# The opening of a transformer block kernel: instructions issued in written order on four engines

## The chip, the cores and the metric

The kernel runs on one core of a Trainium2 chip. A core has five engines with a queue each: PE (TensorE, matrix products into PSUM), DVE (VectorE), ACT (ScalarE), POOL (GpSimd) and SP (which here only issues the DMAs that bring data from HBM into SBUF). Each engine works its queue in the order in which the program was compiled, and an instruction whose inputs or buffers aren't ready holds everything behind it on that engine. The metric is the time of one execution on the device, in microseconds (us); lower is better.

## The reference, cut to what matters

The reference is one layer of a diffusion transformer block on two streams of 256 tokens (context and latent) with 1024 channels. The part that the change touches is the start of the first feed-forward layer:

```
mod = silu(c) @ w_ada + b_ada             # 9 vectors of 1024 for each stream
shift, scale, gate, ... = split(mod, 9)
h = rmsnorm(x) * norm * (1 + scale) + shift
a, b = split(h @ w13, 2)                  # w13: 1024 x 5632
x = x + 0.5 * gate * ((silu(a) * b) @ w2)
```

After it come the rest of this layer, retention and Fourier mixing, the merge, a second feed-forward layer and a final norm. All data are float32.

## The kernel before, in words

Channels lie on the 128 partitions, so the 1024 channels are eight tiles, and the 512 tokens of both streams lie along the free axis. A float32 product is made of three products of rounded numbers (the helper `mm3`, lines 86 to 90): weights and activations are each split into a high part (a cast on ACT, `wh`, `h1h`) and a low part (a subtraction on DVE, `wl`, `h1l`), and PE adds low times high (L88), high times low (L89) and high times high (L90).

The opening (lines 96 to 333) does the following.

- SP loads a unit matrix, the small vectors `sm`, the conditioning vectors `cr`, the tokens `xs` in four DMAs of two channel tiles, and then for each channel tile k two 128x1024 tiles of `w_ada` (`ada`, one for the scale, one for the shift) and the first columns of `w13` (`w`, 128x768).
- The conditioning vectors go through SiLU, are split and are spread over all partitions by products with ones (L158) into `cb`; transposed, they are `ct` (L164, L167).
- The norm: the squares of the eight tiles (L227 on DVE, L229 on ACT) in the four rotating buffers of tag t2k, their sums by products with ones (L231, `st`), a square root on ACT (L216, `sd1q`), a reciprocal on DVE (L218, `rstd1q`), and four products that spread it to all partitions (L238, `rs`), copied by ACT (L242, `rstd`).
- For each channel tile, the scale by DVE: a multiply with a running sum of `ada` with `cb`, once for each stream (L181, `junk`), then L190 (`amul`). The shift by PE: eight transposes of the other `ada` tile (L252, `tr`), two ACT copies (L255, `at`), products with `ct` (L258), an ACT copy (L263, `row`), a product with two columns (L264) and a DVE addition (L265, `mod`).
- Then the tile itself: DVE multiplies it with scale and rstd (L289, `xr`), ACT adds the shift and rounds (L292, `h1h`), DVE makes the low part (L293, `h1l`).
- With that, 18 products for each tile into six accumulators (`acc`, three pairs of hidden units); eight tiles make them complete. `first_mod` (L314) and the loop at L321 trace these steps.

The written order isn't the order of the queues. The program is compiled by a scheduler that simulates the engines and picks, whenever an engine is free in that simulation, a ready instruction. So the queues of all engines were set by it, DMAs included. After the opening come the hidden units from number 3 on (`ffn1_up`, 48 products each, `pa` and `pb`), which need `h1h` and `h1l` of all eight tiles, two loads and splits of `w13` each (L77 to L79), and go on beside the remaining `ada` tiles on DVE.

Of the kernel before, what the change touches and what calls it, by code (L numbers as in the profile page):

```python
# [13 lines left out]
P = 128  # L14
T = 256
# [22 lines left out]
def block_kernel(ctx: ExitStack, tc: tile.TileContext, i: dict, out: bass.AP):  # L38
# [28 lines left out]
    def wtile(t, name):  # L67
        return wp.tile([P, 1024], F32 if t == "wr" else F32R, name=name, tag=t, bufs=4)
# [29 lines left out]
    pools = {}  # L98
    cr = wtile("wr", "cr")[:, :512]
    V.memset(cr, 0.0)  # L100
    nc.sync.dma_start(cr.rearrange("(q r) n -> q r n", r=32)[:, 0, :], i["cc"])
    unit_raw = stp.tile([P, P], F32, name="unit_raw")
    nc.sync.dma_start(unit_raw, i["unit"])
    sm = per.tile([P, N_SMALL], F32, name="sm")
    nc.sync.dma_start(sm, i["smalls"])
    ones = per.tile([P, P], F32, name="ones")
    V.memset(ones, 1.0 / D)
    ones_dv = per.tile([P, P], F32, name="ones_dv")
    V.memset(ones_dv, 1.0 / DV)
# [26 lines left out]
    first_loads(0)  # L136
    first_loads(1)


    pick = stp.tile([P, 512], F32, name="pick")  # L140
    V.memset(pick, 0.0)
    for q in range(4):
        V.memset(pick[32 * q : 32 * q + 1, q * P : (q + 1) * P], 1.0)
    one_f = wtile("wr", "one_f")[:, :P]
    V.memset(one_f, 1.0)
    one_r = wtile("wh", "one_r")[:, :P]
    V.tensor_copy(one_r, one_f)
# [6 lines left out]
    for q in range(4):  # L154
        r = slice(32 * q, 32 * q + 1)
        ps = bank(f"cb{q}")
        for n, c in enumerate(ch):
            PE.matmul(ps, one_r[r, :], c[r, :], start=(n == 0), stop=(n == 1), tile_position=(32 * q, 0))  # L158
        (S.copy if q % 2 else V.tensor_copy)(cb[:, q // 2, (q % 2) * 512 : (q % 2 + 1) * 512], ps)
    ct = stp.tile([P, 2, 4, 32], F32, name="ct")  # L160
    V.memset(ct, 0.0)
# [7 lines left out]
    both = stp.tile([P, 2], F32, name="both")  # L169
    for st in range(2):  # L170
        V.tensor_reduce(
            both[:, st : st + 1], unit_raw.rearrange("p (q r) -> p r q", r=32)[:, st, :],
            axis=mybir.AxisListType.X, op=ALU.add,
        )
# [47 lines left out]

    ps_st = bank("st1")
    for k in range(KT):
        sq = tp.tile([P, 512], F32, name=f"sq1_{k}", tag="t2k", bufs=T2K)
        if k % 3 == 1:
            V.tensor_tensor(sq, xs[k], xs[k], op=ALU.mult)  # L227
        else:
            S.activation(sq, xs[k], AF.Square)  # L229
        for q in range(4):  # L230
            PE.matmul(  # L231
                ps_st[32 * q : 32 * q + 32, :P], ones[:, :32], sq[:, q * P : (q + 1) * P],
                start=(k == 0), stop=(k == KT - 1), skip_group_check=True, tile_position=(0, 32 * q),
            )
# [6 lines left out]
    rstd1 = stp.tile([P, 512], F32, name="rstd1")  # L241
    S.copy(rstd1, ps_st)  # L242

    def ada_pe(n):


        raw = first_ada.pop(n)
        tr = [bank(f"tr{n}_{j}") for j in range(2)]
        at = [stp.tile([P, 512], F32, name=f"at{n}_{j}", tag=f"at{j}") for j in range(2)]
        for j in range(2):  # L250
            for c in range(4):
                PE.transpose(  # L252
                    tr[j][:, c * P : (c + 1) * P], raw[:, (4 * j + c) * P : (4 * j + c + 1) * P], unit_raw
                )
            S.copy(at[j], tr[j])  # L255
        for j in range(2):
# [6 lines left out]
        S.copy(row, tr[1][:, :P])  # L263
        PE.matmul(tr[0][:, :2], row, both, start=True, stop=True)  # L264
        V.tensor_scalar(  # L265
            mod[:, :, n : n + 1].rearrange("p s o -> p (s o)"), tr[0][:, :2],
            sm[:, BIAS + n : BIAS + n + 1], None, op0=ALU.add,
        )

    def modulated(dst, st, s, k, rstd, col, name, engine=None, lo=None):  # L270

        w = rstd.shape[-1]
        if w > T:
            xr = stp.tile([P, 512], F32, name=f"xr{name}", tag="xr", bufs=2)
        else:
            xr = tp.tile([P, 512], F32, name=f"xr{name}", tag="t2k", bufs=T2K)
# [34 lines left out]
        split(gg[0], gg[1], sa)  # L311
        return gg

    def first_mod(k):  # L314
        ada(KT + k)
        ada_pe(k)
        scale_cols(0, k, k + 1)

    first_mod(0)
    acc = [bank(f"acc{m}") for m in range(2 * M1)]  # L320
    for k in range(KT):  # L321
        if k + 2 < KT:
            first_loads(k + 2)
        modulated(h[k], 0, (0, 1), k, rstd1, 0, f"1_{k}")
        n = 2 * M1 * P
        hi, lo = wtile("wh", f"wh0_{k}"), wtile("wl", f"wl0_{k}")
        S.copy(hi[:, :n], first_w[k][:, :n])
        V.tensor_tensor(lo[:, :n], first_w[k][:, :n], f32(hi[:, :n]), op=ALU.subtract)
# [720 lines left out]
```

## Time and profile before

| | |
|---|---|
| Time, median of 3 runs (lowest, highest) | 1023.95 us (1022.84, 1025.29) |
| The profiled execution: its time, its span | 1024.28 us, 1022.5 us |
| PE busy | 983.2 us, 96% of the span |
| DVE, ACT, POOL busy | 661.5 us (65%), 469.1 us (46%), 62.3 us (6%) |
| Chain that ended last, by engine | PE 89%, DVE 4%, ACT 3%, issue 1%, DMA 1% |

The span is what the profiler recorded; the execution's time is 1.78 us longer. PE is the engine that is nearly always busy. The stretches in which it is not are the start, three places between the stages, and the last 10 us. A share of busy time over the whole span doesn't tell what a stage is worth: that is read from the rows of the stage.

### The profile page before, as it was taken

How to read it: one execution, taken by the hardware profiler on the slowest of the kernel's cores; microseconds unless marked ns; L12 is line 12 of the kernel's file. 1: busy time of each engine (PE TensorE's matmuls, PEld its weight loads, DVE VectorE, ACT ScalarE, POOL GpSimd, SP SyncE). 2: the span in 40 equal slices, each digit the busy share in tenths (PEclk: the TensorE clock that was granted, in tenths of full speed). 3: DMA queues.
4: the chain of work that ended last, by engine and by line, in shares of the span. 5: the costliest groups of instructions: out<-in, count | busy, mean ns of one | idle time of the engine just before them, and what ended most of it. 6: DMA issues, size and time to landing. Idle time of an engine off the chain costs nothing.

```text
span 1022.5 us, 16777 instructions
## 1 busy us (share of the span) xinstructions
PE 983.2 (96%) x6792; PEld 907.0 (89%) x6792; DVE 661.5 (65%) x1083; ACT 469.1 (46%) x725; POOL 62.3 (6%) x39
## 2 busy tenths in 40 slices
PE   4899999999999999999999998999999989999996
PEld 3668888888888889899999997999999989999995
DVE  7938999998332434875575637955555767667543
ACT  5444232223422423755476457754445545554541
POOL 0000000000000013100000007000000210000011
PEclk9999999999999999899999999999999999999999
DMA  8727766996232233224132625455666555656651
GB/s 345 246 76 250 226 208 197 317 409 235 83 111 70 86 89 110 83 85 125 60 124 63 201 65 163 125 172 187 197 186 187 165 164 171 186 181 174 185 179 42
DMA packets 49238, 166.84 MB, mean 163 GB/s; under 512 B 5380, under 2 KB 7044, under 8 KB 49160
## 3 DMA queue, kind: packets, MB, share of 16 engines
q1 hardware_dynamic: 49160, 165.77, 50.8%
q8 instruction: 53, 0.87, 0.3%
q14 instruction: 25, 0.20, 0.1%
HBM read 164.70 MB, written 1.05 MB: 162 GB/s over the span
## 4 chain that ended last, share of the span: by engine, by line
PE 89%; DVE 4%; ACT 3%; issue 1%; DMA 1%; POOL 0%; SPq 0%; DVEq 0%; ACTq 0%; POOLq 0%
PE y L88 4%; PE y L89 4%; PE y L90 4%; PE pa L88 3%; PE pa L89 3%; PE pb L89 3%; PE pa L90 3%; PE pb L90 3%; PE pb L88 3%; PE ro L89 2%; PE ro L90 2%; PE ro L88 2%; PE fa L89 2%; PE z L90 2%; PE z L88 2%; PE z L89 2%
## 5 line engine op out<-in xcount | busy, mean ns | idle before, releaser
L79 DVE TENSOR_TENSOR wl<-wr,wh 128x1024 fp32r<-128x1024 f32 (+1 forms) x214 | 249.0, 1164 | 203.0 <-ACT wh L78 202.1
L78 ACT CAST wh<-wr 128x1024 fp32r<-128x1024 f32 (+1 forms) x226 | 226.9, 1005 | 281.6 <-PE y L90 79.2
L181 DVE CUSTOM_DVE_ANT_0 junk<-ada,cb,sm 128x1024 bf16<-128x1024 f32 x96 | 122.8, 1280 | 5.3 <-DMA ada<-in_ada 4.5
L89 PE MATMUL y<-gl,wh 128*128 128x512 f32 (+1 forms) x198 | 72.5, 366 | 0.0
L88 PE MATMUL y<-gh,wl 128*128 128x512 f32 (+1 forms) x198 | 72.4, 366 | 0.0
L90 PE MATMUL y<-gh,wh 128*128 128x512 f32 (+1 forms) x198 | 72.3, 365 | 0.0
L379 POOL TENSOR_TENSOR ssum<-ssum,sq 128x256 f32<-128x256 f32 (+1 forms) x18 | 24.5, 1362 | 736.0 <-ACT sq L378 722.8
L88 PE MATMUL pa<-h1h,wl 128*128 128x512 f32 x152 | 59.2, 390 | 0.0
L89 PE MATMUL pa<-h1l,wh 128*128 128x512 f32 x152 | 59.1, 389 | 0.0
L90 PE MATMUL pa<-h1h,wh 128*128 128x512 f32 x152 | 59.1, 389 | 0.0
L88 PE MATMUL pb<-h1h,wl 128*128 128x512 f32 x152 | 59.1, 389 | 0.0
L89 PE MATMUL pb<-h1l,wh 128*128 128x512 f32 x152 | 59.1, 389 | 0.0
L90 PE MATMUL pb<-h1h,wh 128*128 128x512 f32 x152 | 59.1, 389 | 0.0
L89 PE MATMUL fa<-hxl,wh 128*128 128x258 f32 x176 | 50.9, 289 | 0.0
L88 PE MATMUL fa<-hxh,wl 128*128 128x258 f32 x176 | 50.8, 289 | 0.0
L90 PE MATMUL fa<-hxh,wh 128*128 128x258 f32 x176 | 50.6, 288 | 0.0
L89 PE MATMUL fb<-hxl,wh 128*128 128x258 f32 x176 | 50.1, 284 | 0.0
L89 PE MATMUL z<-g2l,wh 128*128 128x256 f32 x176 | 50.0, 284 | 0.0
L88 PE MATMUL fb<-hxh,wl 128*128 128x258 f32 x176 | 50.0, 284 | 0.0
L90 PE MATMUL fb<-hxh,wh 128*128 128x258 f32 x176 | 49.9, 283 | 0.0
L88 PE MATMUL z<-g2h,wl 128*128 128x256 f32 x176 | 49.8, 283 | 0.0
L90 PE MATMUL z<-g2h,wh 128*128 128x256 f32 x176 | 49.8, 283 | 0.0
(309 smaller groups left out, 2896.5 us busy)
## 6 DMA issues: line engine op xcount, KB each, us to landing
ada<-in_ada SPq DMA_DIRECT2D x72, 512.0 KB, 5.2
wr<-in_w13b SPq DMA_DIRECT2D x44, 512.0 KB, 4.4
wr<-in_w13a SPq DMA_DIRECT2D x38, 512.0 KB, 4.2
wrv<-in_wv SPq DMA_DIRECT2D x16, 512.0 KB, 4.5
wr<-in_wg SPq DMA_DIRECT2D x16, 512.0 KB, 3.8
wr<-in_wgate SPq DMA_DIRECT2D x16, 512.0 KB, 4.4
wr<-in_pret SPq DMA_DIRECT2D x16, 512.0 KB, 3.7
wr<-in_w2b SPq DMA_DIRECT2D x16, 512.0 KB, 3.6
```

The lines of the kernel that those rows point to most:

```text
L78: S.copy(hi[:, :n], raw[:, :n])
L79: (lo_engine or V).tensor_tensor(lo[:, :n], raw[:, :n], f32(hi[:, :n]), op=ALU.subtract)
L88: PE.matmul(o, w[1], a[0], start=start, stop=False)
L89: PE.matmul(o, w[0], a[1], start=False, stop=False)
L90: PE.matmul(o, w[0], a[0], start=False, stop=stop)
L181: V.tensor_tensor_reduce(junk, raw, cb[:, s, :], 1.0, sm[:, BIAS + n : BIAS + n + 1], ALU.mult, ALU.add, mod[:, s, n : n + 1],)
L379: G.tensor_tensor(ssum[0][:, cols], ssum[0][:, cols], sq[:, :w], op=ALU.add)
```

## The change

All of the opening is put under a manual schedule for PE, ACT, DVE and SP: on these four engines its instructions stand in the order in which the code issues them, where before the scheduler chose. What comes after the opening is still placed by the scheduler, which may set single instructions between. The code is written in another order to go with that:

- The loads: the unit matrix, `cr`, `xs`, the first `ada` and `w` tiles, then `sm`, then tile by tile.
- The squares alternate between ACT and DVE and have eight buffers (the four of t2k, and four that belong to tiles used later: at0, at1 and two of xr). The copies of `cb` stand between the first squares; the constant `pick` is written after the squares.
- The steps of a channel tile are functions of their own. For the tile after next no work is done ahead any more: beside the products of tile k, the transposes, rows, scale, weight split and columns of tile k + 1 are issued at fixed places between them.

```diff
+    opening = ExitStack()
+    opening.enter_context(
+        tc.manual_schedule(
+            engines={
+                mybir.EngineType.PE, mybir.EngineType.Activation, mybir.EngineType.DVE, mybir.EngineType.SP
+            }
+        )
+    )
...
+        if k < T2K:
+            sq = tp.tile([P, 512], F32, name=f"sq1_{k}", tag="t2k", bufs=T2K)
+        else:
+            sq = stp.tile([P, 512], F32, name=f"sq1_{k}", tag=f"at{k % 2}" if k < 6 else "xr", bufs=1 + (k > 5))
-        if k % 3 == 1:
+        if k % 2:
             V.tensor_tensor(sq, xs[k], xs[k], op=ALU.mult)
...
+        if k == 1:
+            cb_copy(0, V.tensor_copy)
+            cb_copy(1, S.copy)
...
-    S.copy(rstd1, ps_st)
+    for s in range(2):
+        S.copy(rstd1[:, s * T : (s + 1) * T], ps_st[:, s * T : (s + 1) * T])
...
-    first_mod(0)
+    ada_turn(0)
+    first_scaled(0)
+    first_split(0)
+    ada_rows(0)
+    ada_cols(0)
+    first_shifted(0)
     acc = [bank(f"acc{m}") for m in range(2 * M1)]
     for k in range(KT):
         if k + 2 < KT:
             first_loads(k + 2)
-        modulated(h[k], 0, (0, 1), k, rstd1, 0, f"1_{k}")
...
-        if k + 1 < KT:
-            first_mod(k + 1)
-        for n in range(2 * M1):
-            mm3(acc[n], sl((hi, lo), slice(None), slice(n * P, (n + 1) * P)), h[k], k == 0, k == KT - 1)
+        more = k + 1 < KT
+        if more:
+            ada_turn(k + 1)
+        first_products(k, range(0, 2))
+        if more:
+            ada_rows(k + 1)
+            first_scaled(k + 1)
+            first_split(k + 1)
+        first_products(k, range(2, 4))
+        if more:
+            ada_cols(k + 1)
+            first_shifted(k + 1)
+        first_products(k, range(4, 6))
+    V.memset(ones_dv, 1.0 / DV)
+    opening.close()
     start.close()
```

`ada_turn` holds the transposes and the `at` copies, `ada_rows` the products with `ct` and the `row` copy, `ada_cols` the last product and `mod`; `first_scaled` is `junk` (twice), `amul` and `xr`, `first_split` is `wh` and `wl`, `first_shifted` is `h1h` and then `h1l`.

ACT, from the square roots of the norm to the first `h1h`, before (numbers behind a name are the scheduler's buffer numbers, those directly behind `wh_` the channel tile):

```order
L327 CAST wh_1_354<-w_1_115 128x768
L216 ACTIVATE sd1q<-st_162,eps 128x128
L327 CAST wh_2_420<-w_2_279 128x768
L327 CAST wh_3_486<-w_3_345 128x768
L242 COPY rstd_220<-rs_215 128x512
L255 COPY at_0_244<-tr_0_242 128x512
L255 COPY at_1_245<-tr_1_243 128x512
L255 COPY at_0_298<-tr_0_296 128x512
L263 COPY row_264<-tr_1_243 128x128
L255 COPY at_1_299<-tr_1_297 128x512
L263 COPY row_318<-tr_1_297 128x128
L292 ACTIVATE h1h_222<-xr_0_281,mod 128x256 x2
```

and the same place now:

```order
L242 ACTIVATE sq_4_182<-xs_110 128x512
L242 ACTIVATE sq_6_194<-xs_112 128x512
L226 ACTIVATE sd1q<-st_153,eps 128x128
L266 COPY rstd_217<-rs_216 128x256 x2
L280 COPY at_0_242<-tr_0_240 128x512
L280 COPY at_1_243<-tr_1_241 128x512
L351 CAST wh_0_262<-w_0_118 128x768
L293 COPY row_274<-tr_1_241 128x128
L371 ACTIVATE h1h_224<-xr_0_259,mod 128x256 x2
```

The casts of weight tiles 1 to 3 and the copies for tile 1 have gone from between the norm and the first `h1h`; the cast of tile 0 has come in.

PE, the start of one step (products of tile 3, transposes for tile 4), before:

```order
L252 MATMUL tr_0_494<-unit_raw,ada_409 128x128 x4
L252 MATMUL tr_1_495<-unit_raw,ada_409 128x128 x4
L88 MATMUL acc_269<-h1h_228,wl_3_487 128x512
L88 MATMUL acc_270<-h1h_228,wl_3_487 128x512
L88 MATMUL acc_271<-h1h_228,wl_3_487 128x512
L88 MATMUL acc_272<-h1h_228,wl_3_487 128x512
L88 MATMUL acc_273<-h1h_228,wl_3_487 128x512
L88 MATMUL acc_274<-h1h_228,wl_3_487 128x512
L258 MATMUL tr_1_495<-at_0_496,ct 32x128 x4
L258 MATMUL tr_1_495<-at_1_497,ct 32x128 x4
L89 MATMUL acc_269<-h1l_229,wh_3_486 128x512
L90 MATMUL acc_269<-h1h_228,wh_3_486 128x512
```

and one step now (products of tile 2, transposes for tile 3):

```order
L277 MATMUL tr_0_426<-unit_raw,ada_356 128x128 x4
L277 MATMUL tr_1_427<-unit_raw,ada_356 128x128 x4
L88 MATMUL acc_282<-h1h_228,wl_2_399 128x512
L89 MATMUL acc_282<-h1l_229,wh_2_398 128x512
L90 MATMUL acc_282<-h1h_228,wh_2_398 128x512
L88 MATMUL acc_283<-h1h_228,wl_2_399 128x512
L89 MATMUL acc_283<-h1l_229,wh_2_398 128x512
L90 MATMUL acc_283<-h1h_228,wh_2_398 128x512
L288 MATMUL tr_1_427<-at_0_428,ct 32x128 x4
L288 MATMUL tr_1_427<-at_1_429,ct 32x128 x4
L88 MATMUL acc_284<-h1h_228,wl_2_399 128x512
L89 MATMUL acc_284<-h1l_229,wh_2_398 128x512
```

Before, the last product of the shift (L264) comes after all 18 products of a step, just ahead of the next transposes; now it (L299) comes after the twelfth, with six products behind it.

DVE in one step, before (here the scales of tiles 5 and 6 stand beside the weight split of tile 5 and the `mod` and `h1l` of tile 2):

```order
L190 TENSOR_SCALAR amul<-mod,sm 128x2
L181 ISA junk_0_556,mod<-ada_473,cb,sm 128x1024
L181 ISA mod 128x1
L181 ISA junk_1_558,mod<-ada_473,cb,sm 128x1024
L181 ISA mod 128x1
L265 TENSOR_SCALAR mod<-tr_0_362,sm 128x2
L328 TENSOR_TENSOR wl_5_619<-w_5_477,wh_5_618 128x768
L190 TENSOR_SCALAR amul<-mod,sm 128x2
L181 ISA junk_0_622,mod<-ada_539,cb,sm 128x1024
L181 ISA mod 128x1
L293 SCALAR_TENSOR_TENSOR h1l_227<-xr_2_413,mod,h1h_226 128x256 x2
```

and one step now:

```order
L191 ISA junk_0_588,mod<-ada_486,cb,sm 128x1024
L191 ISA mod 128x1
L191 ISA junk_1_590,mod<-ada_486,cb,sm 128x1024
L191 ISA mod 128x1
L200 TENSOR_SCALAR amul<-mod,sm 128x2
L364 SCALAR_TENSOR_TENSOR xr_5_593<-xs_110,amul,rstd_217 128x256 x2
L352 TENSOR_TENSOR wl_5_597<-w_5_490,wh_5_596 128x768
L300 TENSOR_SCALAR mod<-tr_0_558,sm 128x2
L374 SCALAR_TENSOR_TENSOR h1l_235<-xr_5_593,mod,h1h_234 128x256 x2
```

Every DVE instruction of a step now belongs to the one tile whose products come next, and each step has the same nine rows.

## Rows read from the trace of the kernel before

**Rows 1.** Windows: busy us of each engine, granted clock, DMA share, GB/s.
```profile
0.00:29.15 29.15, 13.88 (x137) 9.94 (x137) 22.03 (x50) 15.30 (x26) 0.21 (x4) 1.00 0.91 351
29.15:74.95 45.80, 41.85 (x283) 31.84 (x283) 29.65 (x63) 17.85 (x36) 0.00 (x0) 1.00 0.45 149
75.00:200.00 125.00, 125.00 (x553) 103.51 (x553) 115.35 (x183) 39.09 (x51) 0.00 (x0) 1.00 0.73 232
```

**Rows 2.** Waits of PE, 0 to 75 us: total, times, longest.
```profile
PE acc L88 <- ACT h1h L292: 4.1, 6, 0.9
PE rs L238 <- DVE rstd1q L218: 3.7, 1, 3.7
```

**Rows 3.** Timeline of PE, opening: start, duration, instruction, idle before.
```profile
15.63 1.23 PE L231 MATMUL st<-sq,ones 128*32 128x128 f32 x16 [1.93 <-ACT sq L229]
20.61 2.08 PE L238 MATMUL rs<-rstd1q,pick 128*128 128x128 f32 x8 [3.74 <-DVE rstd1q L218]
22.48 2.93 PE L252 MATMUL tr<-unit_raw,ada 128*128 128x128 f32 x16
...
29.15 1.66 PE L88 MATMUL acc<-h1h,wl 128*128 128x512 f32 x6 [0.50 <-ACT h1h L292]
```

**Rows 4.** Timeline of ACT, opening.
```profile
6.37 0.63 ACT L229 ACTIVATE sq<-xs 128x512 f32<-128x512 f32 x1 [0.47 <-DMA xs<-in_xs]
7.63 1.15 ACT L229 ACTIVATE sq<-xs 128x512 f32<-128x512 f32 x2 [0.64 <-DMA xs<-in_xs]
...
18.18 0.36 ACT L216 ACTIVATE sd1q<-st,eps 128x128 f32<-128x128 f32 x1
...
28.19 0.91 ACT L292 ACTIVATE h1h<-xr,mod 128x256 fp32r<-128x256 f32 x2
```

**Rows 5.** Timeline of DVE, opening.
```profile
1.74 0.48 DVE L141 MEMSET pick<- 128x512 f32 x1
...
2.74 0.85 DVE L143 MEMSET pick<- 1x128 f32 x4
...
11.88 1.29 DVE L159 COPY cb<-cb 128x512 f32<-128x512 f32 x2 [0.78 <-PE cb L158]
...
18.74 0.95 DVE L328 TENSOR_TENSOR wl<-w,wh 128x768 fp32r<-128x768 f32 x1
19.61 0.94 DVE L218 RECIPROCAL rstd1q<-sd1q 128x128 f32<-128x128 f32 x1
...
27.93 0.22 DVE L265 TENSOR_SCALAR mod<-tr,sm 128x2 f32<-128x2 f32 x1
```

**Rows 6.** Timeline of PE, one step and the end of the steps.
```profile
41.56 1.63 PE L88 MATMUL acc<-h1h,wl 128*128 128x512 f32 x6 [0.65 <-ACT h1h L292]
...
46.73 1.11 PE L252 MATMUL tr<-unit_raw,ada 128*128 128x128 f32 x8
...
74.95 0.47 PE L88 MATMUL pa<-h1h,wl 128*128 128x512 f32 x1
```

**Rows 7.** Timeline of DVE, the parts of a step.
```profile
37.44 1.29 DVE L181 CUSTOM_DVE_ANT_0 junk<-ada,cb,sm 128x1024 bf16<-128x1024 f32 x1
...
38.77 1.28 DVE L181 CUSTOM_DVE_ANT_0 junk<-ada,cb,sm 128x1024 bf16<-128x1024 f32 x1
...
49.12 0.88 DVE L293 SCALAR_TENSOR_TENSOR h1l<-xr,mod,h1h 128x256 fp32r<-128x256 f32 x2
49.91 0.22 DVE L190 TENSOR_SCALAR amul<-mod,sm 128x2 f32<-128x2 f32 x1
50.04 0.88 DVE L289 SCALAR_TENSOR_TENSOR xr<-xs,amul,rstd 128x256 f32<-128x256 f32 x2
```

**Rows 8.** Windows, behind a pause of PE between two stages.
```profile
412.00:416.00 4.00, 3.96 (x16) 3.60 (x17) 4.00 (x6) 1.51 (x3) 2.62 (x1) 0.50 0.25 98
416.00:420.00 4.00, 4.00 (x32) 3.90 (x32) 3.37 (x8) 3.13 (x7) 0.00 (x0) 0.86 0.48 135
```

**Rows 9.** DMA issues, 0 to 60 us: KB each, median us to landing.
```profile
w<-in_w13a SPq DMA_DIRECT2D x8, 384.0 KB, 8.3
```

More of the change, by code (lines that the diff above doesn't have):

```diff
@@ L98, in block_kernel @@
     pools = {}
+    unit_raw = stp.tile([P, P], F32, name="unit_raw")
+    nc.sync.dma_start(unit_raw, i["unit"])
     cr = wtile("wr", "cr")[:, :512]
@@ L101, in block_kernel @@
     nc.sync.dma_start(cr.rearrange("(q r) n -> q r n", r=32)[:, 0, :], i["cc"])
[L102 to L109, printed above, removed]
     eps = per.tile([P, 1], F32, name="eps")
@@ L113, in block_kernel @@
     S.activation(warm, eps, AF.Silu)
+    ones = per.tile([P, P], F32, name="ones")
+    V.memset(ones, 1.0 / D)
+    one_f = wtile("wr", "one_f")[:, :P]
+    V.memset(one_f, 1.0)
+    one_r = wtile("wh", "one_r")[:, :P]
+    V.tensor_copy(one_r, one_f)
+    ct = stp.tile([P, 2, 4, 32], F32, name="ct")
+    V.memset(ct, 0.0)
+    both = stp.tile([P, 2], F32, name="both")
+    for st in range(2):
+        V.tensor_reduce(
+            both[:, st : st + 1], unit_raw.rearrange("p (q r) -> p r q", r=32)[:, st, :],
+            axis=mybir.AxisListType.X, op=ALU.add,
+        )
+    sm = per.tile([P, N_SMALL], F32, name="sm")
+    ones_dv = per.tile([P, P], F32, name="ones_dv")
     mod = per.tile([P, 2, 72], F32, name="mod")
@@ L136, in block_kernel @@
     first_loads(0)
+    nc.sync.dma_start(sm, i["smalls"])
     first_loads(1)
[L140 to L147, printed above, removed]
     cb = adp.tile([P, 2, D], F32, name="cb")
@@ L153, in block_kernel @@
     S.activation(warm, cr[:, :1], AF.Sqrt, bias=eps, scale=0.0)
[L154 to L161, printed above, removed]
     ps = bank("ct")
@@ L167, in block_kernel, with cb_copy @@
         V.tensor_copy(ct[:, :, :, st], picked[:, st, :, :, 0])
[L169 to L174, printed above, removed]
+    cb_ps = []
+    for q in range(4):
+        cb_ps.append(bank(f"cb{q}"))
+    for n, c in enumerate(ch):
+        for q in range(4):
+            r = slice(32 * q, 32 * q + 1)
+            PE.matmul(
+                cb_ps[q], one_r[r, :], c[r, :], start=(n == 0), stop=(n == 1), tile_position=(32 * q, 0)
+            )
+    def cb_copy(q, op):
+        op(cb[:, q // 2, (q % 2) * 512 : (q % 2 + 1) * 512], cb_ps[q])
     def ada(n, streams=(0, 1)):
@@ L224, in block_kernel @@
     for k in range(KT):
-        sq = tp.tile([P, 512], F32, name=f"sq1_{k}", tag="t2k", bufs=T2K)
-        if k % 3 == 1:
+        if k < T2K:
[3 more added lines that the diff above has]
+        if k % 2:
             V.tensor_tensor(sq, xs[k], xs[k], op=ALU.mult)
@@ L229, in block_kernel @@
             S.activation(sq, xs[k], AF.Square)
+        if k == 1:
+            cb_copy(0, V.tensor_copy)
+            cb_copy(1, S.copy)
+        if k == 3:
+            cb_copy(2, V.tensor_copy)
+            cb_copy(3, S.copy)
         for q in range(4):
@@ L234, in block_kernel @@
             )
+    pick = stp.tile([P, 512], F32, name="pick")
+    V.memset(pick, 0.0)
+    for q in range(4):
+        V.memset(pick[32 * q : 32 * q + 1, q * P : (q + 1) * P], 1.0)
     r1 = rstd_of(ps_st[:, :P], P, "1q")
     ps_st = bank("rs1")
+    rstd1 = stp.tile([P, 512], F32, name="rstd1")
     for q in range(4):
@@ L240, in block_kernel, with ada_turn @@
         )
-    rstd1 = stp.tile([P, 512], F32, name="rstd1")
-    S.copy(rstd1, ps_st)
-    def ada_pe(n):
+    for s in range(2):
+        S.copy(rstd1[:, s * T : (s + 1) * T], ps_st[:, s * T : (s + 1) * T])
+    turned = {}
+    def ada_turn(n):
         raw = first_ada.pop(n)
@@ L255, in ada_pe, with ada_rows @@
             S.copy(at[j], tr[j])
+        turned[n] = tr, at
+    def ada_rows(n):
+        tr, at = turned[n]
         for j in range(2):
@@ L263, in ada_pe, with ada_cols @@
         S.copy(row, tr[1][:, :P])
+        turned[n] = tr, row
+    def ada_cols(n):
+        tr, row = turned.pop(n)
         PE.matmul(tr[0][:, :2], row, both, start=True, stop=True)
@@ L272, in modulated @@
         w = rstd.shape[-1]
[L273 to L276, printed above, removed]
+        xr = tp.tile([P, 512], F32, name=f"xr{name}", tag="t2k", bufs=T2K)
         if engine is not None:
@@ L312, in gated_unit, with first_split, first_scaled, first_shifted @@
         return gg
-    def first_mod(k):
+    n1 = 2 * M1 * P
+    first_hl = {}
+    def first_split(k):
+        hi, lo = wtile("wh", f"wh0_{k}"), wtile("wl", f"wl0_{k}")
+        S.copy(hi[:, :n1], first_w[k][:, :n1])
+        V.tensor_tensor(lo[:, :n1], first_w[k][:, :n1], f32(hi[:, :n1]), op=ALU.subtract)
+        first_hl[k] = hi, lo
+    xr1 = {}
+    def first_scaled(k):
         ada(KT + k)
-        ada_pe(k)
         scale_cols(0, k, k + 1)
-    first_mod(0)
+        xr1[k] = stp.tile([P, 512], F32, name=f"xr1_{k}", tag="xr", bufs=2)
+        for s in range(2):
+            c = slice(s * T, (s + 1) * T)
+            V.scalar_tensor_tensor(
+                xr1[k][:, c], xs[k][:, c], amul_col(0, s, k), rstd1[:, c], op0=ALU.mult, op1=ALU.mult
+            )
+    def first_shifted(k):
+        for s in range(2):
+            c = slice(s * T, (s + 1) * T)
+            S.activation(h[k][0][:, c], xr1[k][:, c], AF.Identity, bias=shift_col(0, s, k))
+        for s in range(2):
+            c = slice(s * T, (s + 1) * T)
+            V.scalar_tensor_tensor(
+                h[k][1][:, c], xr1[k][:, c], shift_col(0, s, k), f32(h[k][0][:, c]),
+                op0=ALU.add, op1=ALU.subtract,
+            )
+    def first_products(k, ns):
+        w = first_hl[k]
+        for n in ns:
+            mm3(acc[n], sl(w, slice(None), slice(n * P, (n + 1) * P)), h[k], k == 0, k == KT - 1)
+    ada_turn(0)
[4 more added lines that the diff above has]
+    first_shifted(0)
     acc = [bank(f"acc{m}") for m in range(2 * M1)]
@@ L323, in block_kernel @@
             first_loads(k + 2)
-        modulated(h[k], 0, (0, 1), k, rstd1, 0, f"1_{k}")
[L325 to L328, printed above, removed]
-        if k + 1 < KT:
-            first_mod(k + 1)
-        for n in range(2 * M1):
-            mm3(acc[n], sl((hi, lo), slice(None), slice(n * P, (n + 1) * P)), h[k], k == 0, k == KT - 1)
+        more = k + 1 < KT
[13 more added lines that the diff above has]
+    opening.close()
     start.close()
```

## The prediction

> **What bounds the kernel now.** I read the busy times by stretch first, then what PE waited for, then the timelines of PE, ACT and DVE over the opening. PE does nearly all of the work that sets the end: from 75 to 200 us it is busy 125.00 of 125.00 us. In the opening it is not: 13.88 of the first 29.15 us, and 41.85 of the 45.80 us from the first product of the accumulators (29.15) to the first product of hidden unit 3 (74.95) [rows 1, 3, 6]. So what the change can give is PE's idle time before 74.95, and it counts fully only if PE stays busy afterwards. I take 74.95 as the mark: from there PE still has tile 7's 18 products and all 48 of unit 3 to do, and in the new order it has the same when tile 7's products can start.
>
> Two waits make up the idle time. PE waited 3.7 us for the reciprocal of the norm, and six times up to 0.9 us, 4.1 us in total, for `h1h` [rows 2]. The chain to the first product is the norm: the last squares' sums run at 15.63, the square root only at 18.18, the reciprocal at 19.61, the spread at 20.61 [rows 3 to 5]. Between these stand other tiles' work: the reciprocal starts as the weight split of 18.74 ends.
>
> **The first product.** DMA sets the start of the new chain. The first `xs` transfer lets ACT begin at 6.37, the second at 7.63, so they come 1.26 us apart [rows 4], and the fourth at 7.63 + 2 x 1.26 = 10.15. Before, squares 6 and 7 came later because only four buffers held squares, and each waited for PE, and because casts stood ahead of them. With eight buffers and the alternation, the last pair runs at 10.15 on both engines. DVE needs 0.65 us (as its `cb` copies, 1.29 for two [rows 5]; these are now ahead of square 5, in the wait for DMA, and cost nothing as long as the transfers are 1.26 us apart; without that cover, 1.29 us). Squares are done at 10.8, their sums 1.23 later [rows 3] at 12.05, the square root 0.36 later [rows 4] at 12.4. `pick` now stands between square 7 and the reciprocal on DVE: 0.48 + 0.85 = 1.33 [rows 5], from 10.85 to 12.2, beside the sums. The reciprocal, 0.94 [rows 5], ends at 13.4, against 20.55 before.
>
> From the spread to the first product took 29.15 - 20.61 = 8.54 us before. In it PE transposed two tiles ahead of tile 0's rows, 2.93 for 16 [rows 3]; now one, so 1.46 less: 7.08, and the first product starts at 13.4 + 7.1 = 20.5. Does DVE keep up? After the reciprocal it has two scale sums at 1.33 start to start, 0.13, 0.79 for the pair of `xr` [rows 7] and 0.87 for the weight split (18.74 to 19.61, [rows 5]): 13.4 + 5.3 = 18.7 if nothing waits, and `h1h` must start some 0.96 before the first product, at 19.5. That fits with 0.8 us over. Gain so far 29.15 - 20.5 = 8.65 us.
>
> **A step.** Seven steps lie between the first product and the mark. For PE, products, rows and column of one tile took 46.73 - 41.56 = 5.17 without a wait, and eight transposes take 1.11 with their tail, 0.9 without [rows 6]: 6.05 to 6.3. The new order puts transposes, rows and column between the products in three places instead of two; I count 0.1 for that and take 6.2. For DVE, which before had done its scales ahead and now does each tile's own: 2 x 1.33 (37.44 to 38.77) + 0.13 (49.91 to 50.04) + 0.79 (49.12 to 49.91) [rows 7] + 0.87 (weight split) + 0.26 (from `mod` at 27.93 to `h1h` at 28.19) + 0.91 for `h1h` + 0.03 for the handing over + 0.40 for the second half of `h1l` [rows 4, 5, 7] = 6.05. DVE waits for ACT there, and this wait is in the sum; queued behind it are the next tile's scale sums, and for these PE waits one step later. The wait of PE for `h1h` goes, since `mod` no longer comes after the eighteenth product but after the twelfth: six products, about 1.4 us, and the next eight transposes, 0.9, cover 0.26 + 0.91. What is late next is DVE, by 0.15 us less than PE. ACT, busy 17.85 of 45.80 us, has room [rows 1].
>
> So seven steps take 7 x 6.2 = 43.4 where 45.80 passed before: 2.4 us. In the last, the scheduler puts two casts of unit 3 ahead of `h1h` on ACT and their two splits ahead of `h1l` on DVE; PE has 27 products of unit 3 in its queue there, so I count nothing. Ends for a step: 6.05 (both engines' bare sums), which gives 1.05 us more, and 7.0 (PE's 6.05 and the old longest wait of 0.9 kept), 5.6 us less.
>
> **PE's pace after a pause.** Transposes at 22.48 took 0.18 us each, at 46.73 0.14 with the tail in it [rows 3, 6], though the granted clock reads 1.00 in both stretches [rows 1]; so PE's early work is slow in the old chain, too, and these durations are in my sum. What isn't is the pace of tile 0's products, which now come after a shorter burst of PE work. [...]
>
> **After the mark.** PE's queue is the same but for a few swaps, and the three loads, splits and scales next to come stand as far from the mark as before, so the rest shifts as a whole. DVE is the cover: it is busy 115.35 of 125 us there [rows 1], with PE never waiting. If it came to the mark later than PE by more than its lead, the difference would be lost; at worst I count 2 us.
>
> **The sum.** 8.65 + 2.4 - 1.0 = 10.05 us. The profiled execution took 1024.28 us, so 1014.2; it lies 0.33 above the median of the three runs, 1023.95, so 1013.9.
>
> **Rivals.**
> - *Clean steps*: no slow products and 6.05 a step: 8.65 + (45.80 - 42.35) = 12.1 us, about 1011.9. It is the near end of the forecast's own range, with the other at 1016.5 (steps of 6.5 us or one more microsecond in the norm chain).
> - *The old pace stays*: written order couples the four engines in each step. Column and `mod` wait behind `wl`, this behind `wh`, this behind the `row` copy, this behind PE's fourth row of work. If one hand-over more than I see is on the path, steps take 7.0: 8.65 + 45.80 - 49.0 = 5.5 us, less 1.0 for the pace: 1019.5. For it speaks that each wait now holds all behind it; against it that the two sums, 6.05 and 6.2, each have their waits in them.
> - *Slow clock at the first products*: PE comes to them with a shorter burst behind it, runs them at the lower of its two levels, and gets the higher one back only while it works, as behind the pause between two stages [rows 8]. They cost 2.6 instead of 1.0: 1015.5. For it: the transposes at 22.48 were slow. Against it: the products at 29.15 were not. [...]
> - *The gain is eaten after the mark*: PE reaches unit 4 earlier than DVE has split its weights. PE never waits there now, and DVE's queue shifts with it; if DVE had to catch up all its idle time of the stretch, 125 - 115.35 = 9.65 us [rows 1], before PE went on, next to nothing would remain: about 1023.5.
> - *Slower: a late load in every step.* SP's queue is in written order too: the weight tile of a step stands behind two `ada` loads that wait for buffers, and `wh` on ACT holds `h1h` behind it. From 7.6 us a step the change loses, as 20.5 + 7 x 7.6 + 1.0 = 74.7. With the load 3 us late each time a step takes 9.2: 20.5 + 64.4 + 1.0 = 85.9, 11 us behind the mark, 1034.9. Against it: a weight load takes 8.3 us in the median [rows 9] in the crowded start, and by the buffer counts (six `ada`, four `w`) it is issued about three steps, 18 us, before its cast.
>
> That the change doesn't do what it says can be left out as a rival: the queues of the four engines stand in written order in the rows shown.
>
> **How the numbers follow.** Forecast with clean steps, 1010.5 to 1016.5: 0.64. Slow clock, at its upper edge: 0.08. Old pace: 0.16. Eaten: 0.06. Slower: 0.06. The range takes the first three, from 1010.5 (12.1 us and half a microsecond of the norm chain, with the last of the pace's cost gone, and another microsecond) to 1019.5: 0.83 with what the edges lose. A measurement of this kernel can tell 0.2%, 2.05 us, from no change. Faster by more: the first three, 0.88, and a part of eaten, 0.02: 0.90. Within: 0.04. Slower: 0.06.
>
> **What would show it.** In the changed kernel's timeline: reciprocal near 12.4 to 13.4, first accumulator product near 20.5, then steps of 6.2 us with PE's waits for `h1h` gone, the first product of unit 3 behind one of tile 7 near 65, PE busy without a break from there to 200 us. Squares that still wait for PE, steps of 7 us, or waits of PE for `wl` between 75 and 200 us would make the prediction wrong.

## The result, and the profile after

The changed kernel took 1013.78 us in the median of four runs (1011.73 to 1015.47), the kernel before 1023.39 in four runs on the same chip (1022.61 to 1025.29): a ratio of 0.9902, with a 95% interval of 0.9879 to 0.9926. The profiled execution of the changed kernel was the slowest of its four, 1015.47 us with a span of 1013.7; before it was 1024.28.

PE's wait for the reciprocal [rows 2] fell from 3.7 to 1.5 us, and its six waits for `h1h`, 4.1 us in all, became one of 0.7. Waits of PE from 0 to 75 us after the change (total, times, longest):

```profile
PE rs L262 <- DVE rstd1q L228: 1.5, 1, 1.5
PE st L250 <- ACT sq L242: 1.4, 3, 0.8
PE acc L88 <- ACT h1h L371: 0.7, 1, 0.7
```

The windows that answer to [rows 1], cut at the first product (21.94) and at the mark (66.40):

```profile
0.00:21.94 21.94, 13.50 (x118) 9.62 (x119) 14.48 (x36) 11.63 (x21) 0.20 (x4) 1.00 0.88 330
21.94:66.40 44.46, 43.77 (x303) 33.28 (x301) 39.14 (x78) 22.58 (x45) 0.00 (x0) 1.00 0.55 186
67.00:192.00 125.00, 125.00 (x553) 103.50 (x552) 116.32 (x187) 37.68 (x50) 0.00 (x0) 1.00 0.74 249
```

PE's busy time up to the first product is nearly the same (13.50 and 13.88), while the stretch is 7.21 us shorter. DVE has 39.14 us of work between first product and mark, where it had 29.65: it no longer works ahead. From 67 to 192 us PE doesn't pause, as before.

PE's timeline, where [rows 3, 6] stood (start, duration, instruction, idle before):

```profile
13.97 2.08 PE L262 MATMUL rs<-rstd1q,pick 128*128 128x128 f32 x8 [1.48 <-DVE rstd1q L228]
15.84 1.92 PE L277 MATMUL tr<-unit_raw,ada 128*128 128x128 f32 x8
18.43 1.08 PE L288 MATMUL tr<-at,ct 128*32 128x128 f32 x16 [0.67 <-ACT at L280]
...
21.94 0.78 PE L88 MATMUL acc<-h1h,wl 128*128 128x512 f32 x1
22.51 0.63 PE L89 MATMUL acc<-h1l,wh 128*128 128x512 f32 x1
...
29.73 0.48 PE L88 MATMUL acc<-h1h,wl 128*128 128x512 f32 x1
...
66.40 0.50 PE L88 MATMUL acc<-h1h,wl 128*128 128x512 f32 x1 [0.69 <-ACT h1h L371]
66.74 0.39 PE L88 MATMUL pa<-h1h,wl 128*128 128x512 f32 x1
```

Tile 0's products follow each other at 0.43 us (22.51, 22.94, 23.37 and so on), later ones at 0.23, and eight transposes take 1.92 at 15.84 and 1.03 in the steps: PE runs at about half pace until about 25.8 us, while the granted clock of that stretch reads 1.00 (the experiments on PE's pace come back to this). The tiles' first products stand at 21.94, 29.73, 35.78, 41.79, 47.82, 53.98, 60.20 and 66.40: one step of 7.79 us, then 6.05, 6.01, 6.03, 6.16, 6.22 and 6.20.

ACT and DVE at the places of [rows 4, 5, 7]: ACT's last square and square root, and the end of the steps; then DVE's reciprocal and one step.

```profile
10.73 0.63 ACT L242 ACTIVATE sq<-xs 128x512 f32<-128x512 f32 x1 [0.62 <-DMA xs<-in_xs]
...
12.56 0.37 ACT L226 ACTIVATE sd1q<-st,eps 128x128 f32<-128x128 f32 x1 [1.20 <-PE st L250]
...
63.54 2.00 ACT L78 CAST wh<-wr 128x1024 fp32r<-128x1024 f32 x2
65.44 0.91 ACT L371 ACTIVATE h1h<-xr,mod 128x256 fp32r<-128x256 f32 x2
```

```profile
12.96 0.95 DVE L228 RECIPROCAL rstd1q<-sd1q 128x128 f32<-128x128 f32 x1
...
41.05 0.88 DVE L374 SCALAR_TENSOR_TENSOR h1l<-xr,mod,h1h 128x256 fp32r<-128x256 f32 x2 [0.58 <-ACT h1h L371]
41.85 1.28 DVE L191 CUSTOM_DVE_ANT_0 junk<-ada,cb,sm 128x1024 bf16<-128x1024 f32 x1
...
46.44 0.21 DVE L300 TENSOR_SCALAR mod<-tr,sm 128x2 f32<-128x2 f32 x1
47.22 0.88 DVE L374 SCALAR_TENSOR_TENSOR h1l<-xr,mod,h1h 128x256 fp32r<-128x256 f32 x2 [0.58 <-ACT h1h L371]
48.03 1.28 DVE L191 CUSTOM_DVE_ANT_0 junk<-ada,cb,sm 128x1024 bf16<-128x1024 f32 x1
```

DVE's step is 6.18 us long (41.85 to 48.03): 5.60 without a gap, and 0.58 in which `h1l` waits for `h1h`. PE's own work in a step is 6.02.

### The profile page after: what moved, and what is told of

Its sections match the earlier page's. It is cut to its first block, busy times and chain, and to the rows that moved or that the text cites. A ratio compares the mean times of both kernels' runs of the same rounds, so it can differ in the third digit from the quotient of the medians.

```text
span 1013.7 us, 16779 instructions
## 1 busy us (share of the span) xinstructions
PE 984.4 (97%) x6792; PEld 907.9 (90%) x6792; DVE 663.9 (65%) x1084; ACT 469.4 (46%) x725; POOL 62.4 (6%) x39
## 4 chain that ended last, share of the span: by engine, by line
PE 91%; DVE 4%; ACT 2%; DMA 1%; issue 1%; POOL 0%; DVEq 0%; SPq 0%; ACTq 0%; POOLq 0%
PE y L88 4%; PE y L89 4%; PE y L90 4%; PE pa L89 3%; PE pb L89 3%; PE pa L88 3%; PE pb L88 3%; PE pb L90 3%; PE pa L90 3%; PE ro L89 2%; PE ro L90 2%; PE ro L88 2%; PE fa L89 2%; PE z L90 2%; PE z L89 2%; PE z L88 2%
```

## The experiments

Each run has its place in this table, from its profiled execution. The mark is the first product of tile 7 or of unit 3, whichever comes first, so that PE still has all of both to do there; the median is over all its runs, the ratio is to the kernel before on the same chip (the chips differ between groups of runs, so ratios are the better comparison). Times are in us.

| | spread starts | to first product | seven steps | mark | profiled time less mark | median us | ratio (95%) |
|---|---|---|---|---|---|---|---|
| before | 20.61 | 8.54 | 45.80 | 74.95 | 949.33 | 1023.39 | |
| after | 13.97 | 7.97 | 44.46 | 66.40 | 949.07 | 1013.78 | 0.9902 (0.9879, 0.9926) |
| after again | 13.52 | 7.97 | 44.31 | 65.80 | 948.79 | 1014.59 | 0.9893 (0.9877, 0.9909) |
| no manual schedule | 19.59 | 10.25 | 47.36 | 77.20 | 948.22 | 1026.26 | 1.0011 (0.9997, 1.0024) |
| manual, old text | 14.68 | 12.06 | 53.54 | 80.28 | 947.50 | 1028.20 | 1.0041 (1.0028, 1.0054) |
| four buffers | 14.04 | 7.29 | 43.45 | 64.78 | 948.87 | 1013.88 | 0.9900 (0.9885, 0.9915) |
| busy PE | 14.20 | 6.10 | 43.46 | 63.76 | 948.73 | 1012.08 | 0.9882 (0.9867, 0.9897) |
| manual norm | 14.56 | 9.51 | 47.15 | 71.22 | 948.20 | 1020.99 | 0.9964 (0.9951, 0.9977) |
| manual steps | 19.15 | 7.23 | 43.48 | 69.86 | 949.42 | 1018.24 | 0.9935 (0.9913, 0.9957) |
| sum in the wait | 13.50 | 6.82 | 44.35 | 64.67 | 948.99 | 1013.41 | 0.9892 (0.9870, 0.9914) |
| all three | 14.30 | 5.93 | 44.06 | 64.29 | 949.54 | 1013.24 | 0.9886 (0.9868, 0.9904) |
| half split | 14.15 | 7.97 | 43.91 | 66.03 | 949.03 | 1014.25 | 0.9893 (0.9878, 0.9908) |
| busy PE, half split | 15.22 | 5.54 | 42.55 | 63.31 | 948.96 | 1010.23 | 0.9861 (0.9847, 0.9875) |
| the same, early casts | 14.00 | 5.54 | 41.66 | 61.20 | 948.91 | 1010.47 | 0.9863 (0.9849, 0.9877) |

**Is it the text or the schedule?** The new text without the manual schedule, and the old text under it:

```diff
-    opening.enter_context(tc.manual_schedule(engines={...}))     # first run
-    opening.close()
...
+    opening.enter_context(tc.manual_schedule(engines={...}))     # second run, around before's opening
```

> The new text with its eight buffers, but without the manual schedule: the scheduler sets the queues again. Theory (the gain comes from the queues' order, and the text alone doesn't set it): the scheduler sets casts and a second tile's transposes between the norm and the first product again; first product 27 to 29 us, steps of 6.5 to 7 us, first product of hidden unit 3 (the mark) at 72 to 75 us instead of 66.4, time 1020 to 1024. Rival (the new text carries the gain by the order in which it is written): mark at 66 to 68, time 1013 to 1015.5.

> The old text, with all of the opening under the manual schedule. Theory (both are needed): the norm is free of other tiles' work, first product at 22 to 24, but PE stands still in each step between transposes, rows and column, which stand together ahead of the products (0.65 for the second copy, 0.35 for the row copy), so steps of about 7 us, mark at 70 to 73, time 1018 to 1021. Rival (manual order alone is enough): mark at 66 to 67.5, time 1013 to 1015.5. Second rival (a serial step, each engine behind the other): steps of 8 us and more, mark past 78, slower than before.

Neither does it alone. Without the manual schedule nothing is gained (the interval of its ratio holds 1), which is worse than expected (mark at 77.20 us, 1026.26 us). DVE's timeline there shows what the scheduler put ahead of the reciprocal: scale sums, the first of which waits for a load, and a weight split.

```profile
15.30 1.28 DVE L183 CUSTOM_DVE_ANT_0 junk<-ada,cb,sm 128x1024 bf16<-128x1024 f32 x1 [2.08 <-DMA sm<-in_smalls]
...
16.51 0.95 DVE L344 TENSOR_TENSOR wl<-w,wh 128x768 fp32r<-128x768 f32 x1
17.38 1.28 DVE L183 CUSTOM_DVE_ANT_0 junk<-ada,cb,sm 128x1024 bf16<-128x1024 f32 x1
...
18.59 0.95 DVE L220 RECIPROCAL rstd1q<-sd1q 128x128 f32<-128x128 f32 x1
```

The old text in written order has the early spread (14.68), 5.9 us sooner than before, and loses 3.5 us on the way to the first product and 7.7 in the steps, where PE waits for ACT's copies every time. Some 2.8 of the 7.7 are another thing, PE's pace in tile 0's products (first step 10.10 us, the next 7.34; see below). What the theory gave this run (a gain) was wrong; its second rival had the mark (80.28) and the loss right, though the steps are 7.65 us in the mean and not 8. PE's waits from 0 to 81 us:

```profile
PE tr L266 <- ACT at L263: 9.3, 8, 3.7
...
PE tr L272 <- ACT row L271: 3.5, 8, 0.4
```

**Which half of the opening?** The manual schedule closed after the norm, or opened after it.

```diff
     for s in range(2):
         S.copy(rstd1[:, s * T : (s + 1) * T], ps_st[:, s * T : (s + 1) * T])
+    opening.close()      # manual norm; for manual steps it is opened here instead
```

> The changed kernel with its manual schedule closed after the copies of rstd1, so that the norm's half is issued as written and the eight steps are left to the scheduler. Theory A (the written order of the steps is needed as well, because it also keeps the first tiles' casts and the second tile's sums off the way to the first product): rs near 14, but the first product at 24-28 and steps of 6.5-7, mark 70-75, time 1018-1024. Theory B (the norm's half carries the gain): first product 21-23, steps near 6.3, mark 66-68, time 1014-1017.

> The changed kernel with its manual schedule opened only after the copies of rstd1: the norm's half is left to the scheduler, the eight steps are issued as written. Theory A (the steps' half carries the gain): first product 21-23, steps 6.0-6.2, mark 65-67.5, time 1013-1015. Theory B (the norm's half is needed, since the scheduler lets casts and the sums of later tiles go ahead of squares and rstd): rs near 19.6 as in the run without a manual schedule, first product 27-30, mark 71-74, time 1020-1022.

```profile
14.56 2.08 PE L262 MATMUL rs<-rstd1q,pick 128*128 128x128 f32 x8 [1.48 <-DVE rstd1q L228]
...
24.07 2.93 PE L88 MATMUL acc<-h1h,wl 128*128 128x512 f32 x6 [0.42 <-ACT h1h L372]
```

```profile
19.15 2.08 PE L254 MATMUL rs<-rstd1q,pick 128*128 128x128 f32 x8 [6.26 <-DVE amul L192]
...
26.38 0.50 PE L88 MATMUL acc<-h1h,wl 128*128 128x512 f32 x1 [0.45 <-ACT h1h L371]
```

The first fence is the manual norm, the second the manual steps. Theory A holds for the first (mark 71.22, 1020.99 us); the second lies between its two theories, a little better than B (mark 69.86, 1018.24). Against the run without a manual schedule, writing the norm moves the spread from 19.59 to 14.56; writing what follows moves spread to first product from 10.25 to 7.23 and the steps from 47.36 to 43.48. The marks come 5.98 and 7.34 sooner; together 13.3 where both at once give 10.8 (77.20 to 66.40). Most of that difference is PE's pace. Tile 0's products are slow without the manual schedule, in the manual norm and after the change; in the manual steps the pace had risen before them (0.50 us at 26.38, 0.78 at 21.94 after the change). Against the execution with four buffers below, where it had risen too, both at once give 12.4 (77.20 to 64.78). In the same way some 1.6 us of the 3.9 that the steps seem to gain are the pace: the scheduler's steps took 45.80 before, where tile 0's products weren't slow.

**The buffers.** All squares back in the four buffers of t2k, all else as changed.

```diff
-        if k < T2K:
-            sq = tp.tile([P, 512], F32, name=f"sq1_{k}", tag="t2k", bufs=T2K)
-        else:
-            sq = stp.tile([P, 512], F32, name=f"sq1_{k}", tag=f"at{k % 2}" if k < 6 else "xr", bufs=1 + (k > 5))
+        sq = tp.tile([P, 512], F32, name=f"sq1_{k}", tag="t2k", bufs=T2K)
```

> The changed kernel, with the squares back in four buffers. Theory (the squares now come one transfer apart, and PE has summed square k long before square k + 4 is due): nothing, square 4 still starts with its transfer at 9.5, first product 21.9 and mark 66.4 within 0.3 us, time 1013.8 within the noise. Rival (the buffers carry part of the gain, as ACT waited 1.99 us for PE before): the last squares 1 to 2 us later, mark at 67.5 to 68.4, time 1015 to 1016.

The eight buffers give nothing that can be measured: with four, the last squares still start when `xs` has landed, and the median is 1013.88. This execution also shows that PE's pace isn't the same each time. The second tile's transposes took 1.07 here and 1.95 after the change, with the same work ahead of them on PE:

```profile
10.80 0.63 ACT L239 ACTIVATE sq<-xs 128x512 f32<-128x512 f32 x1 [0.60 <-DMA xs<-in_xs]
```

```profile
19.94 1.07 PE L274 MATMUL tr<-unit_raw,ada 128*128 128x128 f32 x8
21.33 0.49 PE L88 MATMUL acc<-h1h,wl 128*128 128x512 f32 x1 [0.32 <-ACT h1h L368]
```

**PE's pace.** Seventeen products of ones with ones into an unused bank, among the sums of the squares and before the first products.

```diff
+    pw = bank("pw")
+    def busy(n):
+        for _ in range(n):
+            PE.matmul(pw[:, :P], ones, ones, start=True, stop=True)
+    busy(6)
...
+        busy((0, 1, 0, 2, 0, 1, 0, 4)[k])
```

> The changed kernel, with 17 products of ones with ones into an unused bank where PE stood idle before the first accumulator product (six at the start, the rest behind the sums of squares, behind the transposes of tile 0 and behind its rows). Theory (PE's early work is slow because PE stood idle before): transposes of tile 0 and 1 from 1.9 to 1.0 us, rows from 1.08 to 0.65, products of tile 0 from 0.43 to 0.23 start to start, first step 6.1 instead of 7.8, first product at 19.5 to 21, mark at 62 to 64, time 1009.5 to 1011.5. Rival (the early work is slow for another reason, such as first use or DMA traffic): the same durations as without, mark at 66.4 to 67.5 since the added products can only delay.

```profile
14.20 1.16 PE L270 MATMUL rs<-rstd1q,pick 128*128 128x128 f32 x8 [0.39 <-DVE rstd1q L235]
...
20.30 0.50 PE L88 MATMUL acc<-h1h,wl 128*128 128x512 f32 x1 [0.89 <-ACT h1h L379]
...
63.76 0.50 PE L88 MATMUL acc<-h1h,wl 128*128 128x512 f32 x1 [0.68 <-ACT h1h L379]
```

The pace theory held: the spread takes 1.16 instead of 2.08, the first product comes 6.10 us behind its start instead of 7.97, and no product of 512 columns into the accumulators runs at 0.43. From spread to mark it is 49.56 us, against 52.43 after the change and 50.74 in the execution with four buffers. So by this comparison the slow pace cost 2.9 us in the profiled execution after the change, and less in others. The time missed its forecast (1009.5 to 1011.5): 1012.08 us, 1.8 below the four-buffer kernel on the same chip. The four executions of the one lie below the four of the other (at most 1013.09, at least 1013.39), but the intervals of the two ratios overlap, so the gain of the dummies alone isn't measured well.

In this run the slow pace can be set beside the granted clock, which falls to 0.50 at 8.67 us and reads 1.00 again from 12.04. The windows are as in [rows 1]; behind them are two rows of PE's sums of the squares:

```profile
5.00:8.67 3.67, 2.40 (x40) 1.30 (x42) 2.87 (x7) 2.88 (x6) 0.00 (x0) 1.00 1.01 385
8.67:12.04 3.37, 3.37 (x38) 2.17 (x26) 2.28 (x5) 1.40 (x3) 0.00 (x0) 0.50 1.00 382
12.04:20.00 7.96, 6.60 (x73) 5.38 (x72) 6.34 (x15) 3.64 (x9) 0.00 (x0) 1.00 1.03 406
```

```profile
10.34 1.08 PE L257 MATMUL st<-sq,ones 128*32 128x128 f32 x16
...
12.08 0.64 PE L257 MATMUL st<-sq,ones 128*32 128x128 f32 x16
```

At a granted clock of 0.50 one square's sums take 1.08 us, as they do after the change; at 1.00 they take 0.64. Eight of the fourteen profiled executions have a stretch at 0.50 in the opening, and the durations in it are the long ones: in the manual norm it runs from 23.67 to 27.03 and holds tile 0's first products (2.93 for six at 24.07); with the old text it runs from about 25.7 to 32.7 and holds products that follow each other at 0.43 (27.31 to 32.43). So in these stretches the slow pace goes with a granted clock of 0.50. But the column reads 1.00 at the start of every trace, over slow durations too (here the first dummies, 2.93 for 12 instructions at 1.60, where eight take 1.16 at 12.66). A slow stretch with which a trace begins, as after the change, is seen in the durations alone; that it is the lower clock too is my estimate from the equal 1.08 us, and no run shows it.

When the pace rises differs between executions with the same work on PE: the first steps are 7.79 and 7.60 us in the two profiled executions of the changed kernel, and 6.34 in the kernel with four buffers.

**DVE's wait of 0.58.** First the next tile's first scale sum was put into it, alone and in a version that had also the dummies and unit 3's casts behind tile 7's `h1h`.

```diff
+            if k + 2 < KT:
+                first_sum(k + 2, 0)       # between ada_cols (mod) and first_shifted (h1h, h1l)
```

> The changed kernel with each tile's first scale sum, which needs nothing of the step it is in, written one step earlier on VectorE, between mod and h1l, where VectorE waits 0.58 us for h1h. Theory (VectorE is the bound of a step, 6.18 with that wait in it, PE's own work 6.02): steps 6.02 all through, first product unchanged, mark 0.5-1.2 us earlier at the same pace of the first step, time 1012.5-1013.5. Rival (the wait is slack and PE's own work is the bound): steps and mark unchanged within 0.2, time 1013.5-1014. Second rival (the sum put there delays h1l and with it the step): mark 1-4 us later, time 1015-1018.

> The changed kernel with three edits: dummy products that keep PE at work ahead of the first product (as in the busy-PE run, 1012.08), the sum moved into VectorE's wait, and hidden unit 3's weight loads and splits written inside the opening behind h1h of tile 7, so that ScalarE's two casts no longer stand ahead of it. Theory: first product 20.3, steps 6.02, no wait of 0.68 ahead of tile 7's products, mark 62.2-62.6, time 1010.5-1011.2. Rival (the two casts only move their 2.0 us behind the mark, where hidden unit 3's first product waits for them): mark 62.5, the first product of unit 3 as late as before, time 1012.

The steps became longer, 6.29 us in the mean in both (transposes at 26.39 and, five steps on, at 57.86 in the first), so the theory was wrong. The second rival had the mechanism right and the size too large: seven steps of 44.35, 0.9 us more than the 43.45 of the execution with four buffers, whose pace also rose early. The first run's 1013.41, which lies in the theory's range, comes with that early rise (first product at 20.32). The version with all three took 1013.24 us where 1010.5 to 1011.2 was forecast, and isn't better than the dummies alone (ratios 0.9886 and 0.9882). DVE's timeline of the first run shows a new ring:

```profile
37.10 0.96 DVE L352 TENSOR_TENSOR wl<-w,wh 128x768 fp32r<-128x768 f32 x1 [0.83 <-ACT wh L351]
...
38.11 1.28 DVE L360 CUSTOM_DVE_ANT_0 junk<-ada,cb,sm 128x1024 bf16<-128x1024 f32 x1
...
39.31 0.88 DVE L385 SCALAR_TENSOR_TENSOR h1l<-xr,mod,h1h 128x256 fp32r<-128x256 f32 x2
```

A sum of 1.28 in a wait of 0.58 makes `h1l` late: it starts 1.33 us behind `mod` (37.98 to 39.31) instead of 0.78 (46.44 to 47.22 after the change). As the rows read, PE's products, the rows behind them, ACT's copy and its cast come late with it, and DVE then waits 0.83 for the cast. So next only what fits went there, half of the weight split.

```diff
-        V.tensor_tensor(lo[:, :n1], first_w[k][:, :n1], f32(hi[:, :n1]), op=ALU.subtract)
+        first_low(k, 0)                   # columns 0 to 383
...
             ada_cols(k + 1)
+            first_low(k + 1, 1)           # columns 384 to 767
             first_shifted(k + 1)
```

> The changed kernel with the subtraction of the weight split (wl, 0.95 on VectorE) cut into two halves of 384 columns, the second of which is written between mod and h1l, where VectorE waits 0.58 us for h1h. Theory (a ring of mod, h1h, h1l and 5.6 us of VectorE's own work sets the step at 6.18, and only work as short as the wait, about 0.5, goes into it without delaying h1l): steps 5.95-6.05 in place of 6.16-6.22, mark 0.6-1.1 us earlier than the changed kernel's at the same pace of the first products, time 0.5-1.2 us below the changed kernel on the same chip. Rival (the wait is slack and PE bounds): steps 6.16-6.22, same time.

> The busy-PE kernel with the halved weight split. Theory: first product 20.3, steps 5.95-6.05, mark 62.7-63.1, time 0.7-1.2 us below the busy-PE kernel's 1012.08, 1010.9-1011.4. Rival: as the busy-PE kernel, mark 63.8, 1012.

> As the run before, with hidden unit 3's weight casts written behind h1h of tile 7, so that tile 7's products don't wait 0.68 for them and all stand ahead of unit 3's. Theory: mark 62.1-62.5, time 0.4-0.7 below that run. Rival (the casts' 2.0 us then delay the gate of units 0 to 2 instead, as the run with the sum moved left 949.54 behind its mark in place of 949.07): same time within 0.3.

> The changed kernel itself, beside the three others on one chip: 1013-1014.5, first product 21-22 with the pace of the first products differing from one execution to the next.

DVE in a step, and PE's transposes in two steps following each other, both with dummies and half split:

```profile
43.11 0.22 DVE L308 TENSOR_SCALAR mod<-tr,sm 128x2 f32<-128x2 f32 x1
43.25 0.55 DVE L366 TENSOR_TENSOR wl<-w,wh 128x384 fp32r<-128x384 f32 x1
43.91 0.89 DVE L387 SCALAR_TENSOR_TENSOR h1l<-xr,mod,h1h 128x256 fp32r<-128x256 f32 x2
```

```profile
44.39 1.03 PE L285 MATMUL tr<-unit_raw,ada 128*128 128x128 f32 x8
...
50.41 1.03 PE L285 MATMUL tr<-unit_raw,ada 128*128 128x128 f32 x8
```

The wait is filled, and the second to the sixth step take 6.01 to 6.02 us each in all three versions (the first has the pace in it, the last has no transposes). So DVE's ring was the bound of the later steps, and PE is now. Alone this moves the seven steps by 0.4 to 0.55 us, and the medians (1014.25 and 1014.59 for the changed kernel beside it) can't tell them apart; the 0.5 to 1.2 us that were forecast aren't shown. With the dummies it also shortens the way to the first product, from 6.10 to 5.54, because half a split less stands ahead of tile 0's `mod`. That version took 1010.23 us (1009.58 to 1012.27), 4.4 below the changed kernel on the same chip, whose five executions ran from 1012.34 to 1015.59; its ratio of 0.9861 is the lowest here. That is more than the two parts gave by themselves (1.8 and 0.3 us), and why stays open.

The dummies have a price when the pace rises late. In this version's profiled execution, the slowest of its four, they ran slow among the sums of the squares, and the square root came at 13.81 us, where it came at 12.79 with the dummies alone and at 12.56 after the change:

```profile
12.09 0.80 PE L171 MATMUL pw<-ones 128*128 128x128 f32 x2
12.81 0.92 PE L257 MATMUL st<-sq,ones 128*32 128x128 f32 x16
```

```profile
13.81 0.37 ACT L233 ACTIVATE sd1q<-st,eps 128x128 f32<-128x128 f32 x1 [2.45 <-PE st L257]
```

With unit 3's casts behind `h1h` of tile 7, PE has no wait ahead of tile 7:

```profile
61.20 0.44 PE L88 MATMUL acc<-h1h,wl 128*128 128x512 f32 x1
```

From first product to mark it is 0.89 us less. The medians, 1010.47 and 1010.23, don't show it: the time is the same within 0.3, as the rival had it, but not for the rival's reason, since what follows the mark is as long (948.91 and 948.96). Whether it is worth anything stays open.

## Why the prediction was right

The forecast was 1013.9 and its range 1010.5 to 1019.5; the time was 1013.78. The mechanism was as put (the idle time of PE ahead of the mark goes, the rest shifts), with sizes that were off in both directions. That the median lies 0.12 us from the forecast is luck: terms of the sum were off by up to 0.9 us, and the profiled execution, 1015.47, lies 1.3 above the 1014.2 that the sum gave for it.

- **The norm chain.** Predicted: reciprocal done at 13.4, 13.91 measured. The fourth `xs` transfer landed at 10.73 instead of 10.15; behind it the chain held. The reason given for the late squares of before was half wrong: a cast on ACT and a weight split on DVE stood ahead of squares 6 and 7 (13.73 and 14.60 us), but the wait for PE (1.99 us) is that of an earlier square, at 10.78, and in written order the four buffers cost nothing.
- **Spread to first product.** Predicted 7.08, measured 7.97, because PE's half pace covers all of this stretch. The durations that I took from before contain a faster part: 2.93 for 16 transposes there, 1.92 for eight here. With the full pace (busy PE) it is 6.10. So the first product came at 21.94, a gain of 7.21 instead of 8.65. This is the term that was most off. The check that DVE keeps up was summed wrongly (its terms make 4.45, not 5.3), which changed nothing.
- **PE's pace in tile 0's products.** Counted at 1.0, an estimate that no run shows; measured 7.79 - 6.02 = 1.77, between it and the 2.6 of the slow-clock rival (4 x 0.50 + 4 x 0.14, what PE lost in the two windows of [rows 8]). With the 0.89 of the point above the pace cost 2.66 more than the rest of the sum holds, which is the slow-clock rival's size, at two places: in the profiled execution that rival's slow products were there beside the forecast's own mechanism. The row at 29.15 in before [rows 3], without slow products, was the wrong one to judge by, since what PE had done ahead of it was another thing, and so was the granted clock of 1.00, which these traces show over slow durations too (1.92 for eight transposes at 15.84 after the change).
- **The steps.** Predicted 43.4 + 1.0, measured 44.46. The two bounds were the other way round: PE's own work is 6.02 and DVE's ring 6.18, not PE 6.2 and DVE 6.05. Splitting the step between the products costs PE nothing, where I had 0.1 for it, and DVE's ring is 0.13 longer than my sum, since `xr` now waits for the `amul` just ahead of it (0.27 from start to start instead of 0.13).
- **The last step.** The casts were counted at nothing, as 27 products of unit 3 were in PE's queue. They are, but behind one product of tile 7 (66.40), which waits 0.69 us for `h1h`. That the step still took 6.20 is luck: it has no transposes, 0.8 us less work for PE, which I had counted in. Without the wait it took 5.22 (the run with early casts).
- **After the mark.** Profiled time less mark is 949.07 against 949.33, and between 947.5 and 949.54 in the fourteen executions of the table: what is gained ahead of the mark arrives at the end. The rival in which it is eaten falls, and so do that of the old pace and that of the late load, as steps of 6.0 to 6.2 leave no room for them. The 1016.5 given as the upper end with clean steps doesn't follow from its terms: steps of 6.5 make 1016.0, a microsecond more in the norm 1014.9.

The mark moved by 8.55 us instead of 10.05 in the profiled execution, which was the slowest of its four. The medians differ by 9.61. Executions of this program differ by more than 3 us. One likely part is that PE's pace rises at different times: the executions after the change and with four buffers, with the same work on PE, have first products at 21.94 and 21.33 and seven steps of 44.46 and 43.45. The two kept traces of the changed kernel itself differ by 0.15 in the seven steps, so for one program it isn't shown that this makes the difference.

## What to carry to other kernels

A written order is worth as much as the text it follows: the same manual schedule lost 4 us with the old text and gained 10 with the new one, and the new text without it gained nothing. Write the longest chain without other tiles' work in it, let each step's hand-overs lie under the products of the tile before, and fill a wait only with work that is no longer than the wait (a sum of 1.28 us in a wait of 0.58 made the steps 6.29). Where PE starts behind idle time, cheap products ahead of the chain are worth trying (the spread took 1.16 us with them, 2.08 without); those that stand in the chain's own queue can delay it (the square root came at 13.81 us in one execution with them, at 12.56 after the change).

## What the runs showed of the hardware

PE ran at about half pace, 0.43 us from product to product of 512 columns where later it is 0.23, and 1.92 for eight transposes where later it is 1.03, in a stretch whose granted clock reads 1.00 (after the change). In eight other executions slow durations stand where the column reads 0.50, as the 1.08 us for one square's sums in the busy-PE run, which take 0.64 at 1.00. At the start of every trace here the column reads 1.00, over slow durations too; whether the clock was the lower one there isn't shown. With added products of ones with ones the full pace was there from 12.0 us on in the busy-PE run (after a first rise and a fall at 8.7), and from about 13.5 in the profiled execution with the half split; without them, after the change, from about 25.8.
